# A two-layer mixer network on one core: zeroed weights on another engine, row factors one iteration later, two stores on another queue, and output tokens in chunks of 512, 384 and 256

## The chip, the core and the metric

The kernel runs on one core of a Trainium2 chip. The time is that of the whole program on the device, in microseconds (us). A core has TensorE (PE, matrix multiplications, with its weight loads shown apart as PEld), VectorE (DVE), ScalarE (ACT), GpSimd (POOL) and SyncE (SP), which here issues the transfers. Each of them works through its own list of instructions in order; they wait for one another by semaphores. TensorE's clock has two levels, 1.2 and 2.4 GHz; the profile gives the granted clock of a stretch as a share of the upper one (0.50 is the lower level).

## The reference

Two layers work on 128 context tokens and 1024 latent tokens of width 1024; inside a layer the width is 2048 for `u` and 2048 for `z`. Layer 0 mixes tokens by a Fourier transform, layer 1 by a gated linear recurrence in both directions:

```python
def _layer(x, cond, p, kind, h0):
    shift, scale, gate = _ada(cond, w_ada, b_ada)
    h = _rmsnorm(x, norm_g) * (1.0 + scale) + shift
    u, z = jnp.split(h @ w_in, 2, axis=-1)
    if kind == 0:
        y = _fourier_mix(u, p["w_fmix"], p["b_fmix"])   # real part of an FFT over tokens and 256 channels, then 8 blocks of 256x256
    else:
        ...                                             # convolution, gates, scans in both directions
    out = (y * jax.nn.silu(z)) @ w_out
    return x + gate * out, state
```

After the second layer comes a last RMS norm with the gain `final_g`, which scales each token by one factor.

## The kernel before

Activations lie channel by token: 128 channels on the partitions, 1152 tokens (128 + 1024) along the row. A matrix multiplication in fp32 is three with fp32r operands: `split` makes of a tile a high part (an ACT copy, L227) and a low part (a DVE subtraction, L230), and `mm3` (L240 to L242) multiplies high by high, high by low and low by high.

The program runs through these stages: 0 to 95 us the tables of the Fourier transform; 95 to about 250 us the loop over g (8 groups of 256 channels); then `z` of layer 0 for 16 row blocks and its output stage; then layer 1; from about 1275 us its output stage, which ends the program.

**The loop over g.** `uweights(g + 1)` loads two halves uL and uR of 512 KB (L833, L835), makes their sum `e` and difference (written over uL) on DVE (L838, L839) and splits both into e.h, e.l, o.h, o.l. `umat(g)` multiplies these with the transformed tokens Q into `pu` and copies `pu` out as `uh` (ACT, L870) and `ul` (DVE, L871). `ymat(g - 1)` multiplies the result of the iteration before with two 256x256 blocks (`pa`, which ACT copies to `p`; `qb`), and 16 DVE operations make `y` of `p` and `qb` (L901 to L908), stored as yD (L909). Beside it, at g = 0:

- `prologue()` makes the weights `w8`, which are zero but for some columns, and multiplies them with Q into `nyq` (L797), which goes to `Ucat` (L800) and from there into `pa`.
- `rows()` spreads the tokens' norm factors over the partitions: 9 diagonal tiles `dg` on DVE (L808), three multiplications `rb` (L810), and copies on ACT into the row tile of the same name.
- `norm_stream(c, k)`, 24 times, 4 for each g from 0 to 5: SP loads a tile `nt` of x (L823), POOL scales it with `rb`, shift and scale, and SP stores it to hD (L829). There are 3 buffers for `nt`. The `z` stage loads hD again as `hr`.
- At g = 2, SP stores the vector silT to silD (L928), from where a later load broadcasts it.

An engine's order is the order in which the code calls it, but the tile scheduler reorders what isn't pinned by `keep_in_program_order`. SP is one list: a load behind a store that must wait for POOL waits with it.

**The output stage** (`out_stage`). The tokens are cut into three chunks OC of 384. For each chunk all 16 `g` tiles of 128 channels are loaded as `gr` and split into `gh` and `gl`, and for each of 8 row blocks m the 16 are multiplied with w_out's block in two halves of 8 (tiles `wo`, 512 KB each, split on loading), into one `o` in PSUM. The result times `gate` plus `xr`, the layer's input, is `x` (L1092). Squares are summed over the 8 blocks, three column sums `r` (L1039) are turned into factors (`rsqrt_cols`), three diagonal tiles `dg` (L1045) are spread by one multiplication `b` (L1053), and `to_out` scales and stores the 8 tiles (L1444, L1445). For layer 1 the first 8 steps go through the first half of blocks 0 to 3 and then their second half, so that PE can start before all `g` tiles are there. The split tiles lie in pools of 10 and 26 slots, used in turn.

Of the kernel before, what the change touches and what calls it, by code (L numbers as in the profile page):

```python
# [7 lines left out]
F32 = mybir.dt.float32  # L8
F32R = mybir.dt.float32r
# [10 lines left out]
KD = 8  # L20
DI = 2048
MT = 16
# [3 lines left out]
UC = ((0, 256), (256, 578))  # L26
ENG = {mybir.EngineType.PE, mybir.EngineType.DVE, mybir.EngineType.Activation}
OC = ((0, 384), (384, 768), (768, 1152))
GAP = 3
LB = 30.0  # L30
BO = 60.0
# [156 lines left out]
def body(tc, nc, a):  # L188
# [50 lines left out]
    def mm3(out, wh, wl, xh, xl, first, last):  # L239
        PE.matmul(out, wh, xh, start=first, stop=False)  # L240
        PE.matmul(out, wh, xl, start=False, stop=False)  # L241
        PE.matmul(out, wl, xh, start=False, stop=last)  # L242
# [531 lines left out]
    with pool("us", "right") as up:  # L774
# [6 lines left out]
        def prologue():  # L781

            w8r = up.tile([128, KD, G], F32, name="w8r")
            SY.dma_start(w8r, a["w128"])
            w8f = hl_tiles("w8")[0]
            w8 = w8f.rearrange("p (k n) -> p k n", k=KD)
            zt = up.tile([128, 1024], F32, tag="e", name="zt")
            tc.keep_in_program_order(V.memset(zt, 0.0))
            V.tensor_copy(w8f, zt)
            for o in (0, 32, 64):  # L790
                V.tensor_copy(w8[:, :, o:o + 8], w8r)
                V.tensor_tensor(w8[:, :, o + 8:o + 16], w8r, w8[:, :, 0:8].bitcast(F32), op=ALU.subtract)
            pu = ps2("nyq")
            for i, (lo, hi) in enumerate(UC):
                for k in range(KD):
                    for j in range(2):
                        PE.matmul(pu[i][:, 0:hi - lo], w8[:, k, :], Qc[i][k][j][:, 0, :],  # L797
                                  start=k == 0 and j == 0, stop=k == KD - 1 and j == 1)
                A.copy(Ucat[:, lo:hi], pu[i][:, 0:hi - lo])
                V.tensor_tensor(Ucat[32:64, lo:hi], pu[i][32:64, 0:hi - lo], Ucat[32:64, lo:hi].bitcast(F32), op=ALU.subtract)  # L800
# [113 lines left out]
        for g in range(G):  # L914
            nxt = uweights(g + 1) if g + 1 < G else None
            uv = umat(g, uw)
            if g == 0:
                prologue()
            if prev is not None:
                ymat(g - 1, prev)  # L920
            if g == 0:
                rows()
            for c, k in ns[4 * g:4 * g + 4]:
                norm_stream(c, k)
            prev, uw = uv, nxt
            if g == 2:
                for q in range(2):
                    tc.keep_in_program_order(SY.dma_start(silD[0, q].rearrange("(k p) -> p k", p=128), silT[:, :, q]))  # L928
        zw = {m: wload(a["w_z0"][m], f"wz{m}") for m in range(2)}
        hqb_cm.__exit__(None, None, None)  # L930
        hqa_cm.__exit__(None, None, None)
# [21 lines left out]

    def g_load(layer, c, k, src=None, eng=None):

        lo, hi = OC[c]
        n = c * MT + k
        total = sum(p[1] for p in gpools)
        n %= total
        for p, bufs, rbufs in gpools:  # L960
            if n < bufs:
                break
            n -= bufs
        r = src
        if r is None:
            r = p.tile([128, 384], F32, tag="gr", name=f"gr{layer}{c}{k}", bufs=rbufs)
            SY.dma_start(r, gD[layer][k][:, lo:hi])
        h = p.tile([128, 384], F32R, tag="gh", name=f"gh{layer}{c}{k}", bufs=bufs)
        lw = p.tile([128, 384], F32R, tag="gl", name=f"gl{layer}{c}{k}", bufs=bufs)
        split(r, h, lw, eng)  # L970
        return h, lw

# [54 lines left out]
    def out_stage(layer, op, ow, on_chunk):  # L1027
        order = [(c, m) for c in range(3) for m in range(KD)]
        gt = {}
        pending = []  # L1030
        for k in range(MT):
            gt[0, k] = gt0.get(k) if layer == 0 else g_load(layer, 0, k)

        def norm_steps(c, ssum, xt, last=()):
            def sums():
                pr = ps(f"r{layer}{c}")
                todo = [(t, i) for t in (ssum, *last) for i in range(3)]
                for n, (t, i) in enumerate(todo):
                    PE.matmul(pr[:, 2 * i:2 * i + 2], t[:, i * 128:i * 128 + 128], ones[:, 0:2],  # L1039
                              start=n == 0, stop=n == len(todo) - 1)  # L1040
                r3 = op.tile([128, 3], F32, tag="r3", name=f"r3{layer}{c}", bufs=2)
                rsqrt_cols(r3, pr[:, 0:6:2], op, f"rr{layer}{c}", 3)
                dg = op.tile([128, 384], F32, tag="sq", name=f"dg{layer}{c}", bufs=2)
                for i in range(3):
                    V.tensor_scalar(dg[:, i * 128:i * 128 + 128], ident, r3[:, i:i + 1], None, op0=ALU.mult)  # L1045
                if layer == 1 and c == 2:
                    spread(dg)
                else:
                    pending.append(lambda: spread(dg))

            def spread(dg):
                pb = ps(f"b{layer}{c}")
                PE.matmul(pb[:, 0:384], ones128, dg, start=True, stop=True)  # L1053
                on_chunk(c, xt, pb)
            return sums

        steps = [(c, m, hf) for c, m in order for hf in range(2)]
        if layer == 1:

            steps[0:8] = [(0, m, hf) for hf in range(2) for m in range(4)]  # L1060
        pts = {}
        for n, (c, m, hf) in enumerate(steps):
            lo, hi = OC[c]
            for c2, m2, hf2 in steps[n + 2 if n == 0 else n + 3:n + 4]:
                ow[c2, m2, hf2] = wload(a[f"w_out_{layer}"][m2][:, hf2], f"wo{layer}{c2}{m2}{hf2}")
            if hf == 0:
                pts[m] = ps(f"o{layer}{c}{m}")
            wh, wl = ow.pop((c, m, hf))
            for k8 in range(8):
                k = hf * 8 + k8  # L1070
                ks = slice(k8 * 128, k8 * 128 + 128)
                mm3(pts[m][:, 0:384], wh[:, ks], wl[:, ks], *gt[c, k], k == 0, k == MT - 1)
            if hf == 0:
                continue
            pt = pts.pop(m)
            if m == 0:
                ssum = op.tile([128, 384], F32, tag="ssum", name=f"ssum{layer}{c}", bufs=2)
                xt = []
            xr = op.tile([128, 384], F32, tag="xr", name=f"xr{layer}{c}{m}", bufs=3)
            if layer == 0:  # L1080
                SY.dma_start(xr, a["xT"][m][:, lo:hi])
                add_pos(xr, m, lo, hi)
            else:
                SY.dma_start(xr, x1D[c][m])
            if pending:
                pending.pop(0)()
            if m == KD - 1 and c < 2:
                for k in range(MT):
                    gt[c + 1, k] = g_load(layer, c + 1, k)
            x = op.tile([128, 384], F32, tag="x", name=f"x{layer}{c}{m}", bufs=10)  # L1090
            for s, e, q in segments(lo, hi):
                V.scalar_tensor_tensor(x[:, s - lo:e - lo], pt[:, s - lo:e - lo], gate(layer, m, q), xr[:, s - lo:e - lo],  # L1092
                                       op0=ALU.mult, op1=ALU.add)
            if m == 0:
                A.activation(ssum, x, AF.Square)
            else:
                sq = op.tile([128, 384], F32, tag="sq", name=f"sq{layer}{c}{m}", bufs=2)
                A.activation(sq, x, AF.Square)
                if (layer, c, m) == (1, 2, KD - 1):
                    tail = (sq,)  # L1100
                else:
                    tail = ()
                    V.tensor_tensor(ssum, ssum, sq, op=ALU.add)
            xt.append(x)
            if layer == 0:
                SY.dma_start(x1D[c][m], x)
            if m == KD - 1:
                pending.append(norm_steps(c, ssum, xt, tail))
        return pending
# [327 lines left out]


    with pool("gpa", "right") as ga_, pool("gpb") as gb_, pool("os1") as op:
        gpools[:] = [(ga_, 10, 3), (gb_, 26, 4)]  # L1440
        def to_out(c, xt, pb):
            lo, hi = OC[c]
            for m in range(KD):
                V.scalar_tensor_tensor(xt[m], xt[m], fing[:, m:m + 1], pb[:, 0:384], op0=ALU.mult, op1=ALU.mult)  # L1444
                SY.dma_start(a["yT"][m][:, lo:hi], xt[m])  # L1445

        for step in out_stage(1, op, ow1, to_out):
            step()
# [114 lines left out]
```

## Time and profile before

| | |
|---|---|
| time, median of 3 runs | 1502.44 us (1501.05, 1502.5, 1502.44) |
| profiled execution | 1502.73 us, of which the span of its instructions is 1500.9 |
| PE busy | 1438.3 us, 96% of the span |
| DVE, ACT, POOL busy | 72%, 49%, 9% |
| granted clock of PE, mean | 0.989 |
| moved by DMA | 214.14 MB, 143 GB/s on average |

An engine that is busy all the time sets the time; where PE is this, a change of other engines' work counts only where PE waits for it, or where its clock is low.

### The profile page before, as it was taken

How to read it: one execution, taken by the hardware profiler on the slowest of the kernel's cores; microseconds unless marked ns; L12 is line 12 of the kernel's file. 1: busy time of each engine (PE TensorE's matmuls, PEld its weight loads, DVE VectorE, ACT ScalarE, POOL GpSimd, SP SyncE). 2: the span in 40 equal slices, each digit the busy share in tenths (PEclk: the TensorE clock that was granted, in tenths of full speed). 3: DMA queues.
4: the chain of work that ended last, by engine and by line, in shares of the span. 5: the costliest groups of instructions: out<-in, count | busy, mean ns of one | idle time of the engine just before them, and what ended most of it. 6: DMA issues, size and time to landing. Idle time of an engine off the chain costs nothing. (4 is left out here: it accounts for less than half of the span.)

```text
span 1500.9 us, 21433 instructions
## 1 busy us (share of the span) xinstructions
PE 1438.3 (96%) x8364; PEld 1411.9 (94%) x8364; DVE 1077.3 (72%) x1592; ACT 739.8 (49%) x1109; POOL 128.6 (9%) x148
## 2 busy tenths in 40 slices
PE   3989989999999999999999999999999999999997
PEld 2689889999999999999999999999999999899996
DVE  7886455789864475747888787878787888676453
ACT  6553214322222354426866666666665758354231
POOL 2107570000001001100000000000000000000000
PEclk9999989999999999999999999999999999999998
DMA  7645765877755667631111111111111112786461
GB/s 257 215 152 178 150 216 192 295 249 249 235 196 162 184 186 243 189 127 43 59 59 59 58 59 58 59 59 58 59 59 59 59 59 64 229 278 213 148 189 48
DMA packets 84694, 214.14 MB, mean 143 GB/s; under 512 B 11504, under 2 KB 42736, under 8 KB 84464
## 3 DMA queue, kind: packets, MB, share of 16 engines
q1 hardware_dynamic: 84592, 212.77, 44.1%
q8 instruction: 65, 1.06, 0.3%
q14 instruction: 37, 0.30, 0.1%
HBM read 173.38 MB, written 39.35 MB: 142 GB/s over the span
## 5 line engine op out<-in xcount | busy, mean ns | idle before, releaser
L272 DVE SCALAR_TENSOR_TENSOR sil1j<-wada,sil 128x1024 bf16<-128x1024 f32 x64 | 78.1, 1221 | 9.9 <-DMA wada<-w_ada 9.8
L1278 DVE SCALAR_TENSOR_TENSOR uc<-u,tab,uc 128x1156 f32<-128x1156 f32 (+2 forms) x54 | 69.3, 1288 | 15.7 <-ACT u L1261 14.4
L1337 DVE SCALAR_TENSOR_TENSOR nu<-ga,nu 128x1156 f32<-128x1156 f32 x32 | 43.4, 1358 | 47.1 <-ACT tr L1332 47.1
L1092 DVE SCALAR_TENSOR_TENSOR x<-o,ada,xr 128x128 f32<-128x128 f32 (+1 forms) x64 | 31.6, 513 | 60.1 <-PE o L242 59.6
L1315 ACT ACTIVATE tr<-g,gb 128x386 f32<-128x386 f32 (+1 forms) x96 | 54.7, 584 | 22.0 <-PE g L242 21.0
L227 ACT CAST gh<-gr 128x384 fp32r<-128x384 f32 x80 | 39.7, 511 | 52.4 <-DMA gr<-gD 51.0
L1264 ACT ACTIVATE uc<-u,tab 128x386 f32<-128x386 f32 (+1 forms) x48 | 32.3, 673 | 61.7 <-PE u L242 61.7
L870 ACT CAST uh<-pu 128x256 fp32r<-128x256 f32 (+1 forms) x32 | 12.6, 397 | 100.0 <-PE pu L242 99.7
L230 DVE TENSOR_TENSOR gl<-gr,gh 128x384 fp32r<-128x384 f32 x80 | 42.2, 555 | 26.2 <-ACT gh L227 25.8
L1390 ACT ACTIVATE szz<-zz 128x386 f32<-128x386 f32 (+1 forms) x48 | 23.6, 495 | 72.1 <-PE zz L242 72.1
L771 POOL TENSOR_TENSOR xr<-xr,tab 128x384 f32<-128x384 f32 (+1 forms) x24 | 23.7, 989 | 400.2 <-DMA xr<-xT 353.3
L1315 ACT ACTIVATE ti<-g,gb 128x386 f32<-128x386 f32 (+1 forms) x96 | 51.5, 579 | 5.8 <-PE g L242 5.7
L1360 POOL COPY st<-nu 128x1 f32<-128x1 f32 x16 | 6.8, 426 | 495.5 <-DVE nu L1359 495.4
L1347 DVE SCALAR_TENSOR_TENSOR ti<-ti,uc 128x1156 f32<-128x1156 f32 x32 | 43.4, 1357 | 7.6 <-ACT ti L1315 7.3
L991 ACT ACTIVATE sz<-z 128x384 f32<-128x384 f32 x48 | 23.4, 489 | 49.8 <-PE z L242 34.6
L871 DVE TENSOR_TENSOR ul<-pu,uh 128x256 fp32r<-128x256 f32 (+1 forms) x32 | 14.4, 454 | 41.7 <-ACT uh L870 41.7
L1321 ACT ACTIVATE nu<-tr,sp2p 128x1156 f32<-128x1156 f32 x32 | 43.4, 1357 | 1.2
L1343 DVE SCALAR_TENSOR_TENSOR tr<-ga,tr 128x1156 f32<-128x1156 f32 x32 | 43.5, 1360 | 0.7
L1351 DVE TENSOR_TENSOR ti<-ti,tr 128x1156 f32<-128x1156 f32 x32 | 43.4, 1357 | 0.4
L1325 ACT ACTIVATE ga<-tr,sm 128x1156 f32<-128x1156 f32 x32 | 43.2, 1349 | 0.1
L1362 DVE TENSOR_TENSOR_SCAN nu<-ga,tab,ti 128x1155 f32<-128x1155 f32 x16 | 41.9, 2618 | 0.1
L1359 DVE TENSOR_TENSOR_SCAN nu<-ga,ti 128x1156 f32<-128x1156 f32 x16 | 40.9, 2558 | 0.3
(1812 smaller groups left out, 5550.8 us busy)
## 6 DMA issues: line engine op xcount, KB each, us to landing
wo<-w_out SPq DMA_DIRECT2D x96, 512.0 KB, 4.4
wz<-w_z SPq DMA_DIRECT2D x32, 512.0 KB, 3.6
wada<-w_ada SPq DMA_DIRECT2D x32, 512.0 KB, 4.3
gr<-gD SPq DMA_DIRECT2D x80, 192.0 KB, 4.0
yD<-y SPq DMA_DIRECT2D x16, 576.0 KB, 3.7
zy<-yD SPq DMA_DIRECT2D x16, 576.0 KB, 6.9
wada<-w_adaN SPq DMA_DIRECT2D x16, 512.0 KB, 4.5
wu<-w_u SPq DMA_DIRECT2D x16, 512.0 KB, 3.6
```

The source lines that it names most:

```text
L230: (eng or V).tensor_tensor(lo, src, hi.bitcast(F32), op=ALU.subtract)
L272: V.scalar_tensor_tensor(junk, w, 0.5, sil[:, q, :], op0=ALU.mult, op1=ALU.mult, accum_out=ada[:, layer, mt, q:q + 1])
L1278: V.scalar_tensor_tensor(T["uc", m][:, lo:hi], T[ut][:, lo + t:hi + t], convw[:, m, t:t + 1], T["uc", m][:, lo:hi], op0=ALU.mult, op1=ALU.add)
L1315: A.activation(T[tg, n][:, lo:hi], T["ps", p][:, 0:hi - lo], AF.Tanh, scale=0.5, bias=gb2[:, 2 * d + mat, m:m + 1])
L1321: A.activation(T["nu", n], T["tr", n], AF.Tanh, scale=sp2[:, d, m:m + 1], bias=sp2[:, d, m:m + 1])
L1325: A.activation(T["ga", n], T["tr", n], AF.Exp, scale=sm4[:, d, m:m + 1], bias=sm4[:, d, m:m + 1])
L1337: V.scalar_tensor_tensor(T["nu", n], T["ga", n], 1.0, T["nu", n], op0=ALU.add, op1=ALU.mult)
L1343: V.scalar_tensor_tensor(T["tr", n], T["ga", n], 1.0, T["tr", n], op0=ALU.add, op1=ALU.mult)
L1347: V.scalar_tensor_tensor(T["ti", n], T["ti", n], 1.0, T["uc", m], op0=ALU.add, op1=ALU.mult)
L1351: V.tensor_tensor(ti, ti, T["tr", n], op=ALU.mult)
L1359: V.tensor_tensor_scan(nu, ga, ti, 0.0, ALU.mult, ALU.add)
L1362: V.tensor_tensor_scan(nu[:, 0:L][:, ::-1], ga[:, 0:L][:, ::-1], ti[:, 0:L][:, ::-1], h0[:, 1, m:m + 1], ALU.mult, ALU.add)
```

## The change

It does six things. The zeroing of `w8` and the copies into it move from DVE to ACT, and the tile zt is gone. `rows()` is called at g = 1 and each four `norm_stream` one iteration later. The two silD stores are issued by ACT. In layer 0's output stage the look-ahead of the weights is written another way. In layer 1's output stage the chunks hold 512, 384 and 256 tokens, with tiles 512 wide of which each chunk uses its part; `xr` is loaded in two pieces where a chunk overlaps two of the 384 in which x1D is stored. The pools of split `g` tiles there hold 7 and 20.

```diff
+OUTC = (OC, ((0, 512), (512, 896), (896, 1152)))
...
-            zt = up.tile([128, 1024], F32, tag="e", name="zt")
-            tc.keep_in_program_order(V.memset(zt, 0.0))
-            V.tensor_copy(w8f, zt)
+            A.activation(w8, ident.rearrange("p (o n) -> p o n", o=1).broadcast_to([128, KD, 128]), AF.Copy, scale=0.0)
             for o in (0, 32, 64):
-                V.tensor_copy(w8[:, :, o:o + 8], w8r)
+                A.copy(w8[:, :, o:o + 8], w8r)
...
-            if g == 0:
+            if g == 1:
                 rows()
-            for c, k in ns[4 * g:4 * g + 4]:
+            for c, k in ns[4 * (g - 1):4 * g] if g else ():
                 norm_stream(c, k)
...
-                    tc.keep_in_program_order(SY.dma_start(silD[0, q].rearrange("(k p) -> p k", p=128), silT[:, :, q]))
+                    tc.keep_in_program_order(A.dma_start(silD[0, q].rearrange("(k p) -> p k", p=128), silT[:, :, q]))
...
-        lo, hi = OC[c]
+        lo, hi = OUTC[layer][c]
+        wid, w = 512 if layer else 384, hi - lo
...
-        h = p.tile([128, 384], F32R, tag="gh", name=f"gh{layer}{c}{k}", bufs=bufs)
-        lw = p.tile([128, 384], F32R, tag="gl", name=f"gl{layer}{c}{k}", bufs=bufs)
+        h = p.tile([128, wid], F32R, tag="gh", name=f"gh{layer}{c}{k}", bufs=bufs)[:, 0:w]
+        lw = p.tile([128, wid], F32R, tag="gl", name=f"gl{layer}{c}{k}", bufs=bufs)[:, 0:w]
...
-            for c2, m2, hf2 in steps[n + 2 if n == 0 else n + 3:n + 4]:
+            for c2, m2, hf2 in steps[n + 2 if n == 0 or layer == 0 else n + 3:n + 3 + layer]:
...
-                mm3(pts[m][:, 0:384], wh[:, ks], wl[:, ks], *gt[c, k], k == 0, k == MT - 1)
+                mm3(pts[m][:, 0:hi - lo], wh[:, ks], wl[:, ks], *gt[c, k], k == 0, k == MT - 1)
...
-                SY.dma_start(xr, x1D[c][m])
+                for i, (l, h) in enumerate(OC):
+                    l, h = max(l, lo), min(h, hi)
+                    if l < h:
+                        SY.dma_start(xr[:, l - lo:h - lo], x1D[i][m][:, l - 384 * i:h - 384 * i])
...
-        gpools[:] = [(ga_, 10, 3), (gb_, 26, 4)]
+        gpools[:] = [(ga_, 7, 3), (gb_, 20, 4)]
```

The scheduler settles what this does to the order on each engine; a row gives line, operation, tiles and shape. First DVE in the loop over g, from the low part of e of g = 1 on, before the change:

```order
L230 TENSOR_TENSOR o1l<-uL_1036,o1h 128x1024
L871 TENSOR_TENSOR ul_1_1108<-pu_1_1_1052,uh_1_1107 128x322
L788 MEMSET zt 128x1024
L789 CAST w8h<-zt 128x1024
L791 CAST w8h<-w8r 128x8x8 x3
L838 TENSOR_TENSOR e_1226<-uL_1222,uR_1224 128x1024
L792 TENSOR_TENSOR w8h<-w8r,w8h 128x8x8 x3
L871 TENSOR_TENSOR ul_0_1102<-pu_0_1_1051,uh_0_1101 128x322
L839 TENSOR_TENSOR uL_1222<-uL_1222,uR_1224 128x1024
```

And the same place after it:

```order
L232 TENSOR_TENSOR o1l<-uL_1036,o1h 128x1024
L838 TENSOR_TENSOR e_1166<-uL_1162,uR_1164 128x1024
L871 TENSOR_TENSOR ul_1_1108<-pu_1_1_1052,uh_1_1107 128x322
L792 TENSOR_TENSOR w8h<-w8r,w8h 128x8x8 x3
L839 TENSOR_TENSOR uL_1162<-uL_1162,uR_1164 128x1024
L232 TENSOR_TENSOR e2l<-e_1166,e2h 128x1024
L871 TENSOR_TENSOR ul_0_1102<-pu_0_1_1051,uh_0_1101 128x322
```

The sum `e` of g = 2 now stands directly behind `o1l`, and the subtractions that finish `w8` stand behind it and one `ul`.

PE at the place of `rb`, before the change, between the last `nyq` and the first `pu` of g = 1:

```order
L797 MATMUL nyq_1127<-Qrl,w8h 128x322
L810 MATMUL rb_0_1164<-dg_1166,ones 128x384
L810 MATMUL rb_0_1174<-dg_1176,ones 128x384
L810 MATMUL rb_0_1184<-dg_1186,ones 128x384
L240 MATMUL pu_0_0_1237<-Qoh_170,e1h 128x256
```

And after it, behind the last `qb` of ymat(0):

```order
L242 MATMUL qb_1_1334<-uh_1_1107,Bh 128x322
L243 MATMUL qb_1_1334<-ul_1_1108,Bh 128x322
L244 MATMUL qb_1_1334<-uh_1_1107,Bl 128x322
L810 MATMUL rb_0_1351<-dg_1353,ones 128x384
L810 MATMUL rb_0_1361<-dg_1363,ones 128x384
L810 MATMUL rb_0_1371<-dg_1373,ones 128x384
L242 MATMUL pu_0_0_1424<-Qoh_170,e2h 128x256
```

The three `rb` stand one `umat` and one `ymat` later; on DVE their `dg` stand behind the 16 operations that make `y` of ymat(0).

SP around the loads of g = 7 (uL7, uR7), with the full names of the tiles (hD1_2 belongs to chunk 1 and the channel block 2 of the norm stream), before the change:

```order
L928 DMA silD_117<-silT_196 128x8x1 x2
L829 DMA hD1_2_79<-nt1_4_1843 128x384
L823 DMA nt1_6_1855<-xT 128x384
L829 DMA hD1_2_79<-nt1_5_1849 128x384
L833 DMA uL7_2293<-w_u0 128x1024
L823 DMA nt1_7_1861<-xT 128x384
L823 DMA nt2_0_2056<-xT 128x384
L835 DMA uR7_2295<-w_u0 128x1024
```

And after it:

```order
L829 DMA hD0_3_76<-nt0_7_1619 128x384
L823 DMA nt1_2_1829<-xT 128x384
L829 DMA hD1_0_77<-nt1_0_1817 128x384
L823 DMA nt1_3_1835<-xT 128x384
L833 DMA uL7_2267<-w_u0 128x1024
L829 DMA hD1_0_77<-nt1_1_1823 128x384
L835 DMA uR7_2269<-w_u0 128x1024
L829 DMA hD1_1_78<-nt1_2_1829 128x384
```

silD is gone from SP; on ACT it stands behind the four `p` of ymat(1). uL7 and uR7 stand behind the 9th and 10th hD instead of the 15th.

## Rows read from the trace of the kernel before

**Rows 1.** The page: its head, and PE's busy time.

```profile
span 1500.9 us, 21433 instructions
...
PE 1438.3 (96%) x8364; PEld 1411.9 (94%) x8364; DVE 1077.3 (72%) x1592; ACT 739.8 (49%) x1109; POOL 128.6 (9%) x148
```

**Rows 2.** PE's waits: for whom; us in total, times, longest.

```profile
PE qb L240 <- DVE ul L871: 10.9, 1, 10.9
...
PE nyq L797 <- DVE w8h L792: 2.4, 1, 2.4
...
PE o L241 <- DVE gl L230: 1.5, 1, 1.5
```

**Rows 3.** DVE's timeline, prologue: start us, us, line, operation.

```profile
104.73 0.91 DVE L788 MEMSET zt<- 128x1024 f32 x1 [0.16 <-DVE ul L871]
...
106.82 1.22 DVE L838 TENSOR_TENSOR e<-uL,uR 128x1024 f32<-128x1024 f32 x1
```

**Rows 4.** PE by windows: us, PE busy (matmuls), granted clock, DMA share, GB/s.

```profile
108.58:114.40 5.82, 5.82 (x32) 0.75 0.31 93
114.00:118.00 4.00, 1.74 (x7) 1.00 0.00 0
```

**Rows 5.** Timeline of PE and DVE, `rb` and the end of ymat(0).

```profile
115.85 1.85 DVE L808 TENSOR_SCALAR dg<-tab,rs 128x128 f32<-128x128 f32 x9
...
116.67 2.17 PE L810 MATMUL rb<-dg,ones 128*128 128x384 f32 x6 [2.26 <-DVE dg L808]
...
135.21 0.28 PE L240 MATMUL pu<-Qoh,e2h 128*128 128x256 f32 x1
...
137.79 0.20 DVE L908 TENSOR_TENSOR y<-p,qb 128x63 f32<-128x63 f32 x1
```

**Rows 6.** SP's timeline around silD: start us, us to issue.

```profile
171.62 1.18 SPq L928 DMA_DIRECT2D silD<-silT  x2
...
175.52 0.38 SPq L829 DMA_DIRECT2D hD<-nt  x1
...
185.74 0.38 SPq L835 DMA_DIRECT2D uR<-w_u  x1
```

**Rows 7.** PE by windows, around the long wait.

```profile
176.00:182.00 6.00, 6.00 (x47) 1.00 0.91 23
188.00:200.00 12.00, 5.03 (x22) 0.50 0.61 217
```

**Rows 8.** Tile uL, then line L829: landing, and ns, first and last start.

```profile
DMA to landing us min/median/max: 3.9/4.5/11.2
...
L829 SPq DMA_DIRECT2D hD<-nt x24: 319/326/1022, 124.7 to 221.0; - x24
```

**Rows 9.** Timeline: ACT's `p` of ymat(1), DVE's `e` of g = 6 and 7.

```profile
149.38 1.69 ACT L888 ACTIVATE p<-pa,tab 128x256 f32<-128x256 f32 x4
...
162.49 1.23 DVE L838 TENSOR_TENSOR e<-uL,uR 128x1024 f32<-128x1024 f32 x1 [1.60 <-DMA uR<-w_u]
...
190.70 1.95 DVE L838 TENSOR_TENSOR e<-uL,uR 128x1024 f32<-128x1024 f32 x1 [13.29 <-DMA uR<-w_u]
```

**Rows 10.** PE by windows, start of the last output stage.

```profile
1274.00:1316.00 42.00, 36.73 (x202) 1.00 0.69 222
...
1316.00:1320.00 4.00, 4.00 (x15) 0.57 0.79 230
```

**Rows 11.** PE by windows: matmuls of 512, 256 and 384 columns.

```profile
59.78:62.30 2.52, 2.52 (x12) 1.00 0.95 278
95.04:98.64 3.60, 3.60 (x33) 1.00 0.80 249
...
1340.00:1480.00 140.00, 140.00 (x805) 1.00 0.54 167
```

**Rows 12.** Timeline of the tail: the spread and the final multiplications.

```profile
1491.67 1.65 PE L1053 MATMUL b<-dg,ones 128*128 128x384 f32 x2 [1.94 <-DVE dg L1045]
...
1493.35 4.29 DVE L1444 SCALAR_TENSOR_TENSOR x<-x,tab,b 128x384 f32<-128x384 f32 x8 [1.74 <-PE b L1053]
```

More of the change, by code (lines that the diff above doesn't have):

```diff
@@ L965, in g_load @@
         if r is None:
-            r = p.tile([128, 384], F32, tag="gr", name=f"gr{layer}{c}{k}", bufs=rbufs)
+            r = p.tile([128, wid], F32, tag="gr", name=f"gr{layer}{c}{k}", bufs=rbufs)[:, 0:w]
             SY.dma_start(r, gD[layer][k][:, lo:hi])
-        h = p.tile([128, 384], F32R, tag="gh", name=f"gh{layer}{c}{k}", bufs=bufs)
-        lw = p.tile([128, 384], F32R, tag="gl", name=f"gl{layer}{c}{k}", bufs=bufs)
+        h = p.tile([128, wid], F32R, tag="gh", name=f"gh{layer}{c}{k}", bufs=bufs)[:, 0:w]
+        lw = p.tile([128, wid], F32R, tag="gl", name=f"gl{layer}{c}{k}", bufs=bufs)[:, 0:w]
         split(r, h, lw, eng)
@@ L1029, in out_stage @@
         gt = {}
+        wid = 512 if layer else 384
         pending = []
@@ L1034, in norm_steps @@
         def norm_steps(c, ssum, xt, last=()):
+            nb = xt[0].shape[-1] // 128
             def sums():
                 pr = ps(f"r{layer}{c}")
-                todo = [(t, i) for t in (ssum, *last) for i in range(3)]
+                todo = [(t, i) for t in (ssum, *last) for i in range(nb)]
                 for n, (t, i) in enumerate(todo):
@@ L1040, in sums @@
                               start=n == 0, stop=n == len(todo) - 1)
[L1041 to L1044, printed above, removed]
+                r3 = op.tile([128, nb], F32, tag="r3", name=f"r3{layer}{c}", bufs=2)
+                rsqrt_cols(r3, pr[:, 0:2 * nb:2], op, f"rr{layer}{c}", nb)
+                dg = op.tile([128, wid], F32, tag="sq", name=f"dg{layer}{c}", bufs=2)[:, 0:128 * nb]
+                for i in range(nb):
                     V.tensor_scalar(dg[:, i * 128:i * 128 + 128], ident, r3[:, i:i + 1], None, op0=ALU.mult)
@@ L1052, in spread @@
                 pb = ps(f"b{layer}{c}")
-                PE.matmul(pb[:, 0:384], ones128, dg, start=True, stop=True)
+                PE.matmul(pb[:, 0:128 * nb], ones128, dg, start=True, stop=True)
                 on_chunk(c, xt, pb)
@@ L1062, in out_stage @@
         for n, (c, m, hf) in enumerate(steps):
-            lo, hi = OC[c]
-            for c2, m2, hf2 in steps[n + 2 if n == 0 else n + 3:n + 4]:
+            lo, hi = OUTC[layer][c]
+            for c2, m2, hf2 in steps[n + 2 if n == 0 or layer == 0 else n + 3:n + 3 + layer]:
                 ow[c2, m2, hf2] = wload(a[f"w_out_{layer}"][m2][:, hf2], f"wo{layer}{c2}{m2}{hf2}")
@@ L1076, in out_stage @@
             if m == 0:
-                ssum = op.tile([128, 384], F32, tag="ssum", name=f"ssum{layer}{c}", bufs=2)
+                ssum = op.tile([128, wid], F32, tag="ssum", name=f"ssum{layer}{c}", bufs=2)[:, 0:hi - lo]
                 xt = []
-            xr = op.tile([128, 384], F32, tag="xr", name=f"xr{layer}{c}{m}", bufs=3)
+            xr = op.tile([128, wid], F32, tag="xr", name=f"xr{layer}{c}{m}", bufs=3)[:, 0:hi - lo]
             if layer == 0:
@@ L1089, in out_stage @@
                     gt[c + 1, k] = g_load(layer, c + 1, k)
-            x = op.tile([128, 384], F32, tag="x", name=f"x{layer}{c}{m}", bufs=10)
+            x = op.tile([128, wid], F32, tag="x", name=f"x{layer}{c}{m}", bufs=10)[:, 0:hi - lo]
             for s, e, q in segments(lo, hi):
@@ L1096, in out_stage @@
             else:
-                sq = op.tile([128, 384], F32, tag="sq", name=f"sq{layer}{c}{m}", bufs=2)
+                sq = op.tile([128, wid], F32, tag="sq", name=f"sq{layer}{c}{m}", bufs=2)[:, 0:hi - lo]
                 A.activation(sq, x, AF.Square)
@@ L1439, in body @@
     with pool("gpa", "right") as ga_, pool("gpb") as gb_, pool("os1") as op:
-        gpools[:] = [(ga_, 10, 3), (gb_, 26, 4)]
+        gpools[:] = [(ga_, 7, 3), (gb_, 20, 4)]
         def to_out(c, xt, pb):
-            lo, hi = OC[c]
+            lo, hi = OUTC[1][c]
             for m in range(KD):
-                V.scalar_tensor_tensor(xt[m], xt[m], fing[:, m:m + 1], pb[:, 0:384], op0=ALU.mult, op1=ALU.mult)
+                V.scalar_tensor_tensor(xt[m], xt[m], fing[:, m:m + 1], pb[:, 0:hi - lo], op0=ALU.mult, op1=ALU.mult)
                 SY.dma_start(a["yT"][m][:, lo:hi], xt[m])
```

## The prediction

> **What bounds the kernel now.** I read the page first: TensorE (PE) is busy 96% of the 1500.9 us span [rows 1]. Time can only be won where PE waits, or where its clock has dropped after a wait. So the second view is the list of PE's waits [rows 2]. The longest, before `fold`, is the start of the program, which the change leaves alone. Of the rest, 10.9 us before `qb` and 2.4 before `nyq`, and 2.3 before `rb` [rows 5], lie where the change moves instructions. The third view is the table of windows, for the clock around each wait. I then went through the five parts in the order of the program.
>
> The profiled execution took 1502.73 us, which is 1.83 more than its span and 0.3 above the median of the runs, 1502.44. The sum is made against 1502.73.
>
> **1. The zeroed weights (`w8`) go to ScalarE.** `nyq` waits 2.4 us because on VectorE (DVE) the MEMSET at 104.73 and the casts come first and then `e`, 1.22 us from 106.82 [rows 3], which stands ahead of the subtractions that finish `w8h`. From the start of `e` to that of `nyq` at 108.58 [rows 4] it is 1.76 us. In the changed order `e(2)` stands directly behind `o1l`, and one more `ul` of about 0.45 behind it: 2.2 from `e` to `nyq`. `e` can start where the MEMSET does now, at 104.7, if uR(2) has landed, and did not wait for it at 106.82. So `nyq` starts at 106.9 to 108.6; I take 107.4, since a landing near the middle is as likely as one at either end: −1.2. After the wait the 32 `nyq` matmuls ran at a mean clock of 0.75 for 5.82 us [rows 4], against 0.75 × 5.82 = 4.37 at full clock. The 1.45 lost comes back if the shorter wait leaves the clock at its upper level. The row for that is `rb`: 2.3 us of waiting there, and its window still shows 1.00 [rows 4]. The sum takes 1.2 + 1.4 = **−2.6**; bounds −3 and 0 (uR late, clock down as now). ScalarE's new ACTIVATE and copies cost nothing as long as they lie beside DVE's `e`; without that cover they take the MEMSET's place, 0.9.
>
> **2. `rows()` one iteration later.** This takes the 2.3 us before `rb` away and makes another wait. In the new place the 9 `dg` (1.85 us) stand behind the 16 subtractions and additions of ymat(0). PE is through ymat(0)'s `qb` at 135.21, where the next `pu` starts now, and DVE finishes the last `y` at 137.99 [rows 5]. Three `dg` (0.62) follow, so PE waits some 3.4 us. Against the 2.3 removed that is +1.1. After 2.4 us the clock fell, after 2.3 it did not; 3.4 lies beyond both, so I add one such loss, 1.6. Sum **+2.7**, bounds +1 (clock stays) and +4 (the clock is down for the `pu` behind it too). Queued behind `rb` on PE is `pu` for g = 2.
>
> **3. The silD stores leave SP's queue.** This is the large term. SP issues the two stores at 171.62 in 4-byte pieces. uL(7) leaves right behind the store hD at 175.52, and uR(7) only at 185.74, a stand of 10 us [rows 6]. Between 176 and 182 the DMA engines are 0.91 busy and move 23 GB/s [rows 7]. The slowest uL takes 11.2 us to land, where the median is 4.5 [rows 8]. On DVE `e(7)` waits 13.29 us for uR until 190.70 [rows 9], and behind it and `uL` in order stands the `ul` that PE needs: the 10.9 us before `qb`. From 188 to 200 the clock is 0.50 [rows 7]: PE's 5.03 us of matmuls are worth half of that, 2.5 more. Gross −13.4.
>
> Not all of it comes back. The norm stream begins after `rb`. That started at 116.67 [rows 5]; it will at 135.2 + 3.4 − 7.0 = 131.6, the 7.0 being the 2.6 of part 1 and the 2.26 of wait and 2.17 of work that are gone ahead of it. So the stores hD, of which the first of 24 left at 124.7 [rows 8] and the 15th at 175.52 [rows 6], (175.52 − 124.7)/14 = 3.63 us apart, begin 15 us later, at 139.7. In the changed order uR(7) stands behind hD number 10: 139.7 + 9 × 3.63 = 172.4, in time. uR(6) stands behind number 5, at 154.2, and `e(6)`, which waits for it until 162.49 today with PE right behind, runs as early with the median landing of 4.5. But silD now leaves ACT after the four `p` of ymat(1), which end near 151 [rows 9], just ahead of both. If the packets hold up SP's stream as they do now (the 10 us ahead of uR(7)), uR(6) is issued near 164, `e(6)` starts 6 us late, and the clock falls too (2.5): 8.5. If they only share the engines, nothing. Between 0 and 8.5 I take **+4**, in the middle, for no row shows two queues at work at once. Net **−9.4**, bounds −13.4 and −4.9.
>
> The page "DMA: Bandwidth & Descriptors" of the Trainium skill (section "Issuing engines are not separate DMA queues") speaks against this part: transfers started by different engines run on the same 16 DMA engines and interleave, and another issuing engine only saves the time on the sequencer. The trace agrees so far: what is full from 176 to 182 [rows 7] is the engines, while SP needs 1.18 us to issue the two. By that rule the move alone would be worth those 1.18 us, and the crowding would show wherever the packets now are. That is rival A below.
>
> **4. The start of the last output stage.** From 1274 to 1316 PE works 36.73 of 42.00 us, and from 1316 to 1320 the clock is 0.57 [rows 10]: 5.3 of waiting and 1.7 of clock, 7.0 in all. The first 8 steps run the first four row blocks in both halves, 192 matmuls. At 384 columns one takes 140 us / 803 = 0.174 (of the 805 in the window two reach in from before it), at 512 columns 2.52 / 11 = 0.229 [rows 11]. Needed in that time are 8 weight tiles of 512 KB and 16 `g` tiles of 192 KB, 7.3 MB in 33.4 us = 217 GB/s; after, with 16 of 256 KB, 8.4 MB in 44.0 us = 191 GB/s. The stretch moved 222. So the later waits, where a weight or a `g` tile came late, lose their ground. But the first `gl` now stands behind one more DVE instruction of 1.35 us (L1351), which lengthens today's first wait of 1.5 [rows 2] to about 3. Kept: 3 + 0.5. Sum **−3.5**, bounds −6 and 0.
>
> **5. The stage itself and its tail.** 256 columns take 3.60 / 30 = 0.120 [rows 11], so 0.229 + 0.174 + 0.120 = 0.523 stands against 3 × 0.174 = 0.522: **0**, within 0.8. At the two chunk borders 27 instead of 36 slots hold the split `g` tiles. Tiles 11 to 15 of a new chunk must wait until PE has left tiles 0 to 4 of the old one. PE then has 11 × 3 × 0.229 = 7.6 us of the old chunk and 5.7 of the new one ahead, while five splits take under 3 us. So nothing; without that cover one wait of about 2 with the clock down behind it. In the tail everything that is 384 wide becomes 256: the 8 final multiplications 4.29 → 2.86, the spread `b` 1.65 → 1.10, small ones −0.2 [rows 12]. The stores follow the multiplications. Sum **−2.2**, bounds −1.5 and −2.8. The shifted look-ahead of layer 0 moves one pair of DVE rows and nothing on PE: 0.
>
> **Sum.** −2.6 + 2.7 − 9.4 − 3.5 + 0 − 2.2 = −15.0. 1502.73 − 15.0 = 1487.7, less 0.3 for the median: **1487.5 us**.
>
> **Rivals.**
> A, the crowding moves along: silD holds SP's stream up for the full 10 us at its new place, `e(6)` is 6 us late and the clock falls: 8.5 instead of 4, so 1487.5 + 4.5 = 1492; with the dear bound of part 2 (+1.3) and the output stage's start as slow as now (+3.5), 1497. For it: 0.91 busy at 23 GB/s [rows 7], which no change of the issuing engine removes. Against it: today SP's own stores stand behind silD in one queue, and then they don't. Chance 0.25.
> B, clean: no residual in part 3, and 2.5 more at the start of the output stage: 1487.5 − 6.5 = 1481. For it: uR(6) and uR(7) stand behind hD numbers 5 and 10, due at 154.2 and 172.4, ahead of today's issue. Against it: the time of silD, 151. Chance 0.18.
> C, slower: the small packets on a second queue starve SP's stream instead of sharing with it, and `e(6)` waits for uR(6) longer than `e(7)` does now. Everything but part 3 brings −2.6 + 2.7 − 3.5 − 2.2 = −5.6, so slower by 3 us begins where the residual exceeds 13.4 + 5.6 + 3 = 22 us: `e(6)` at about 182 instead of 162.49, hD number 5 at 175 instead of 154.2, a stand of 21 us against 10 now. For it: SP's stream is already at its latest relative to PE at that place, since it begins 15 us later. Against it: silD's crowding lasted from 171.62 to 182 or so, half of that. Above 1505.5; chance 0.09.
> The forecast's own case, 1484 to 1491, has 0.40. The 0.08 left is a time that can't be told from none: A with waits at the borders of the chunks.
>
> 0.2% (3.0 us) is about what a measurement of this kernel can tell from no change. Faster by more than that 0.83 (the forecast, A and B), within it 0.08, slower 0.09. The range, 1478 to 1500, reaches from B with its bounds to the dear end of A and leaves out C, most of the 0.08 and a tail of B.
>
> **What would show it.** PE's waits after: no 10.9 before `qb`; one before `rb`, of 3 to 4 us, behind `y`; `nyq` under 1.6 us. `e(6)` and `e(7)`: their waits for uR tell A from B. SP's gap after uL(7) gone. Output stage: one wait of 3 us at its start, no clock drop at 1316. The final multiplications 2.9 instead of 4.29 us. The prediction is wrong if the norm stream's delay reaches a later consumer (the `hh` of the z stage), or if the borders of the chunks show waits.

## The result, and the profile after

The changed kernel takes 1492.82 us (median of 6 runs, 1489.78 to 1495.96) against 1501.62 for the kernel before, run beside it: a ratio of 0.9946 with a 95% interval of 0.9932 to 0.9961, about 8 us less. The forecast was 1487.5 with a range of 1478 to 1500. The time lies in the range, but not in the forecast's own case, 1484 to 1491: it is what rival A gave, 1492 to 1497. The profiled execution took 1495.83 us and is one of the longer of the six, so its sum below comes to 6.9 less than that of before.

The head of the page, PE's busy time, and the two queues by which transfers went:

```profile
span 1494.0 us, 21452 instructions
...
PE 1435.5 (96%) x8362; PEld 1393.2 (93%) x8362; DVE 1074.9 (72%) x1587; ACT 740.2 (50%) x1113; POOL 125.2 (8%) x148
...
q1 hardware_dynamic: 84816, 212.76, 44.1%
q10 hardware_dynamic: 2080, 0.01, 0.4%
```

The last line is new: ACT's queue, 2080 packets for 0.01 MB. That is silD. PE's waits, as in [rows 2]:

```profile
PE qb L242 <- DVE ul L871: 10.0, 1, 10.0
...
PE rb L810 <- DVE dg L808: 3.3, 1, 3.3
...
PE o L243 <- DVE gl L232: 2.3, 1, 2.3
...
PE nyq L797 <- DVE w8h L792: 0.7, 1, 0.7
```

The wait before `nyq` has gone from 2.4 to 0.7, the one before `rb` is 3.3, the first `gl` of the last stage costs 2.3 instead of 1.5, all near what was forecast. But a wait of 10.0 us before `qb` is still there. It is not the same one: it now belongs to g = 5, behind `e(6)`. DVE's row for it, beside [rows 9]:

```profile
174.05 1.22 DVE L838 TENSOR_TENSOR e<-uL,uR 128x1024 f32<-128x1024 f32 x1 [13.76 <-DMA uR<-w_u]
```

The timeline of ACT's and SP's queues before it, beside [rows 6]:

```profile
149.75 0.39 ACTq L928 DMA_DIRECT2D silD<-silT  x1
...
150.17 0.59 ACTq L928 DMA_DIRECT2D silD<-silT  x1
...
150.80 0.38 SPq L833 DMA_DIRECT2D uL<-w_u  x1
164.58 0.33 SPq L823 DMA_DIRECT2D nt<-xT  x1
...
167.42 0.38 SPq L835 DMA_DIRECT2D uR<-w_u  x1
```

uL(6) leaves just after silD, as the order said, and then SP stands for 13.8 us. What it waits for is in the list of its own waits from 145 to 170, an `nt` buffer whose store hD doesn't finish:

```profile
SPq L823 <- DMA hD<-nt: 14.9, 2, 13.4
```

uR(6) leaves at 167.42; the estimate was 154.2 undisturbed and 164 held up. The windows, beside [rows 7]:

```profile
152.00:160.00 8.00, 8.00 (x62) 1.00 1.05 11
...
174.00:186.00 12.00, 8.94 (x46) 0.62 0.60 211
```

For 8 us the profile gives the engines a busy share of 1.05 while they move 11 GB/s, and behind the wait PE's clock is again low, 0.62 from 174 to 186. The other places, `rb` and the tail, beside [rows 5] and [rows 12], first the timeline, then the window around `rb`:

```profile
131.00 3.17 PE L810 MATMUL rb<-dg,ones 128*128 128x384 f32 x6 [3.29 <-DVE dg L808]
...
1486.65 0.80 PE L1056 MATMUL b<-dg,ones 128*128 128x256 f32 x2 [1.72 <-DVE dg L1048]
...
1487.49 3.22 DVE L1450 SCALAR_TENSOR_TENSOR x<-x,tab,b 128x256 f32<-128x256 f32 x8 [0.89 <-PE b L1056]
```

```profile
131.00:135.00 4.00, 4.00 (x11) 0.63 0.74 260
```

Behind the wait of 3.3 us before `rb` the clock is down in this execution, as the sum had it.

Where the time came from, by the start of the same instruction in both traces:

| first matmul of | before | after | shift | in this part |
|---|---|---|---|---|
| `pu` of g = 0 | 91.94 | 91.69 | −0.25 | −0.25 |
| `pu` of g = 3 (behind `nyq`, `rb`) | 151.72 | 151.14 | −0.58 | −0.33 |
| `z` (end of the loop over g) | 251.50 | 250.48 | −1.02 | −0.44 |
| `o` of the last stage | 1275.32 | 1273.68 | −1.64 | −0.62 |
| the last matmul of `o` | 1487.24 | 1482.96 | −4.28 | −2.64 |
| end of the span | 1500.9 | 1494.0 | −6.9 | −2.6 |

Most of the gain lies in the last output stage and the tail. The part of the loop from g = 3 on, where −9.4 was forecast for silD alone, gave 0.4.

### The profile page after: what moved, and what is told of

Its sections match the earlier page's. It is cut to its first block, busy times and chain, and to the rows that moved or that the text cites. A ratio compares the mean times of both kernels' runs of the same rounds, so it can differ in the third digit from the quotient of the medians.

```text
span 1494.0 us, 21452 instructions
## 1 busy us (share of the span) xinstructions
PE 1435.5 (96%) x8362; PEld 1393.2 (93%) x8362; DVE 1074.9 (72%) x1587; ACT 740.2 (50%) x1113; POOL 125.2 (8%) x148
## 3 DMA queue, kind: packets, MB, share of 16 engines
q10 hardware_dynamic: 2080, 0.01, 0.4%
## 5 line engine op out<-in xcount | busy, mean ns | idle before, releaser
L1098 DVE SCALAR_TENSOR_TENSOR x<-o,ada,xr 128x128 f32<-128x128 f32 (+2 forms) x64 | 31.6, 513 | 53.5 <-PE o L244 53.0
L229 ACT CAST gh<-gr 128x384 fp32r<-128x384 f32 (+2 forms) x80 | 39.4, 510 | 51.7 <-DMA gr<-gD 50.1
L232 DVE TENSOR_TENSOR gl<-gr,gh 128x384 fp32r<-128x384 f32 (+2 forms) x80 | 42.0, 554 | 28.0 <-ACT gh L229 27.8
L870 ACT CAST uh<-pu 128x256 fp32r<-128x256 f32 (+1 forms) x32 | 12.6, 397 | 95.6 <-PE pu L244 95.5
```

## The experiments

Theory P: silD's 2048 pieces of 4 bytes hold up the other transfers wherever and by whichever queue they are issued. Rival N: the norm stream, which begins later, makes uR(6) late. Rival Q: it matters which queue is used. The first four kernels ran on one chip (the kernel before: 1502.84), the next four on another (1502.49), the last four on a third (1498.71). Most runs of one kernel lie within some 5 us of their median, and the chips differ, so ratios to the kernel before on the same chip are compared.

**1. silD in rows.** silT is turned by one small multiplication and stored as 16 rows of 512 bytes.

```diff
-                for q in range(2):
-                    tc.keep_in_program_order(A.dma_start(silD[0, q].rearrange("(k p) -> p k", p=128), silT[:, :, q]))
+                silQ = up.tile([128, 2, KD], F32, name="silQ")
+                A.copy(silQ, silT.rearrange("p k q -> p q k"))
+                silP = ps("silP")
+                PE.matmul(silP[0:16, 0:128], silQ.rearrange("p q k -> p (q k)"), ident, start=True, stop=True)
+                silW = up.tile([128, 384], F32, tag="nt", name="silW", bufs=3)[0:16, 0:128]
+                A.copy(silW, silP[0:16, 0:128])
+                tc.keep_in_program_order(A.dma_start(silD[0].rearrange("q (k p) -> (q k) p", p=128), silW))
```

> The changed kernel with one edit: silT is copied, turned by one small multiplication with the identity on PE and stored as 16 rows of 512 bytes instead of 2048 pieces of 4 bytes, by ACT at the same place. Theory P (the small packets hold up SP's transfers wherever they are issued): the 10.0 us that PE waits before qb in the changed kernel go, and the low clock behind them (about 2.5), so some 12 us less: about 1481, and no uR takes longer than 7 us to land. Rival N (the later norm stream makes uR(6) late, since it stands behind the fifth hD): the wait stays at 8 us or more and the time within 3 us of the changed kernel, 1490 to 1496.

1480.78 us, ratio 0.9859 (0.9846 to 0.9872): 12 us below the changed kernel, as theory P had it (run 11 below, the same kernel once more, comes out less far down). SP's timeline, then a window of PE, then ACT's copy of the turned rows:

```profile
151.17 0.38 SPq L833 DMA_DIRECT2D uL<-w_u  x1
152.66 0.33 SPq L823 DMA_DIRECT2D nt<-xT  x1
...
153.77 0.42 SPq L835 DMA_DIRECT2D uR<-w_u  x1
```

```profile
152.00:160.00 8.00, 8.00 (x61) 1.00 0.91 299
```

```profile
159.67 0.25 ACT L932 COPY silW<-silP 16x128 f32<-16x128 f32 x1 [8.78 <-DMA hD<-nt]
```

In the order of the changed kernel uR(6) leaves at 153.77, half a us from the 154.2 of the prediction, and in the same 8 us 299 GB/s are moved. No wait before `qb` is left. The norm stream is as late as in the changed kernel, so N falls. One thing differs besides the size of the pieces: the rows leave ACT at 160.0 instead of 150, since silW is one of the three `nt` buffers, and the copy into it waits 8.78 us for a store hD to free one (the turn on PE is done at 152). That the moment alone isn't the cure is for runs 2 and 8 to show, with 4-byte stores at 163.8 and 233.9; none stores them at 160 itself.

**2. silD back on SP's queue.**

```diff
-                    tc.keep_in_program_order(A.dma_start(silD[0, q].rearrange("(k p) -> p k", p=128), silT[:, :, q]))
+                    tc.keep_in_program_order(SY.dma_start(silD[0, q].rearrange("(k p) -> p k", p=128), silT[:, :, q]))
```

> The changed kernel with one edit: the two silD stores back on SP's queue, where they now stand between the eighth hD and uL(7). Theory P: uR(6) comes in time, and uL(7) and uR(7) stand behind the crowd as in the kernel before: a wait of 5 to 11 us before the qb that follows e(7), time within 4 us of the changed kernel, 1489 to 1497. Rival Q (it matters that a second queue is used): without it the wait falls below 3 us, time below 1486, or a second queue was milder and the time rises above 1498.

1495.07 us, ratio 0.9954 (0.9936 to 0.9972), not to be told from the changed kernel's 0.9946. SP's timeline and PE's longest wait behind the start:

```profile
163.79 1.17 SPq L928 DMA_DIRECT2D silD<-silT  x2
...
166.09 0.33 SPq L829 DMA_DIRECT2D hD<-nt  x1
177.50 0.33 SPq L823 DMA_DIRECT2D nt<-xT  x1
177.93 0.99 SPq L833 DMA_DIRECT2D uL<-w_u  x1
...
182.04 0.38 SPq L835 DMA_DIRECT2D uR<-w_u  x1
```

```profile
PE qb L242 <- DVE ul L871: 11.0, 1, 11.0
```

The stand is 11.4 us here, at another place, and the victim is uR(7), as in the kernel before: 11.0 us. Whose queue it is makes no difference that shows in the time, so Q falls too, although the stores also leave 14 us later here. The engines are not full during this stand, as the window shows:

```profile
166.00:177.00 11.00, 11.00 (x84) 1.00 0.47 36
```

A share near 1, as in [rows 7], is thus not needed for SP to stand; the few GB/s are common to both.

**3. `rows()` and the norm stream back in their old iterations,** silD on ACT.

```diff
-            if g == 1:
+            if g == 0:
                 rows()
-            for c, k in ns[4 * (g - 1):4 * g] if g else ():
+            for c, k in ns[4 * g:4 * g + 4]:
```

> The changed kernel with rows() at g = 0 again and the norm stream back in its old iterations; silD stays on ACT. Theory P: the wait of about 10 us stays, since uL(6) and uR(6) are still issued behind silD, and only the dearer wait before rb is won back, 2.7 us: about 1490. Rival N: with the norm stream 13 to 15 us earlier uR(6) and uR(7) come in time, the long wait goes and the time is about 1480.

1493.33 us (12 runs, 1490.61 to 1505.14), ratio 0.9948 (0.9931 to 0.9965). N is out once more: uR(6) still leaves only at 166.54, and from 152 to 160 the engines move 27 GB/s. But the 2.7 didn't come either. PE's waits:

```profile
PE qb L242 <- DVE ul L871: 7.7, 1, 7.7
PE rb L810 <- DVE dg L808: 3.8, 1, 3.8
```

The wait before `qb` is shorter, and the one before `rb` at its old place is 3.8, not 2.26. `nyq` is over sooner here, and PE comes to `rb` sooner.

**4. Three chunks of 384 in the last stage again.**

```diff
-OUTC = (OC, ((0, 512), (512, 896), (896, 1152)))
+OUTC = (OC, OC)
...
-        gpools[:] = [(ga_, 7, 3), (gb_, 20, 4)]
+        gpools[:] = [(ga_, 10, 3), (gb_, 26, 4)]
```

> The changed kernel with the last output stage in three chunks of 384 and pools of 10 and 26 again. Theory: the profiles of before and after put 2.7 us between the start of this stage and its last o and 2.6 in the tail, so 5.3 slower: about 1498. Rival (the stage's gain depends on what comes before it and the tail hides part of it): less than 2.5 us slower, below 1495.5.

1497.8 us, ratio 0.9967 (0.9955 to 0.9978), against 0.9946: about 3 more, between theory and rival, and with these intervals undecided. In its profile the stage and tail take 5.7 us more than in that of the changed kernel (1270.92 to 1496.9, against 1273.68 to 1494.0), hence runs 9 and 10.

**5. silD in rows, in the kernel before** (the edit of run 1, for the stores on SP). It changes queue and moment too: the rows leave ACT at 160.6, where the pieces left SP at 171.62.

> The kernel before with silD turned by PE and stored as 16 rows of 512 bytes on ACT's queue, nothing else. Theory P: the 10.9 us before qb and the low clock behind them go, about 13 us: 1488 to 1491. Rival (the wait before e(7) has its own cause in SP's order of hD, nt and uR(7), and silD only shares it): less than 8 us, above 1494.

1490.27 us, ratio 0.993 (0.991 to 0.9949): the 10.9 us wait and the low clock behind it are worth 10.5 (0.7% of 1502; 8 to 13 by the interval) with the rest of the kernel left as it was. Its profile has no wait before `qb`. By run 2 and the changed kernel, queue and moment alone bring no such gain.

**6. silD in rows, `rows()` and the norm stream back** (the edits of 1 and 3).

> silD in rows as in the first experiment, and rows() with the norm stream back at g = 0. Theory R (the move of rows() is about even, since the earlier nyq only lengthens the wait before rb at its old place): the wait before rb 3.5 to 4 us, time within 2.5 us of the first experiment, 1478.5 to 1483.5. Rival, by the sum as it stood in the prediction (+2.7 for the move): 2.7 faster, about 1478.

1484.62 us, ratio 0.9881 (0.986 to 0.9903). That is above both expectations. Beside run 1 (0.9859) the move of `rows()` would win some 3 us, beside run 11, the same kernel on another chip (0.9891), it would lose 1.5: undecided, and a loss of 2.7 shows in neither. The wait before `rb` is 3.6 in its profile.

**7. `dg` made early:** as run 1, with the nine `dg` at g = 0 and the three `rb` at g = 1.

```diff
+        dgs = {}
+        def row_diags():
+            for c in range(3):
+                dgs[c] = up.tile([128, 384], F32, tag="nt", name=f"dg{c}", bufs=3)
...
         def rows():
...
+                dg = dgs[c]
...
             if g == 0:
                 prologue()
+                row_diags()
```

> silD in rows, rows() at g = 1, but its nine dg made on DVE right behind nyq's Ucat at g = 0, so that they are there when PE comes to rb. Theory: the 3.3 us before rb go, and with them the low clock in rb and the first pu behind it (about 1.7 of PE's time): some 5 us below the first experiment, about 1476. Rival (the nine dg, 1.8 us, now delay uL and o2l or the copies of pu at g = 1, and a wait comes back there): within 2 us of the first experiment.

1480.62 us, ratio 0.9859 (0.9834 to 0.9884), the same ratio as run 1, on another chip: undecided by time. PE's timeline shows that the wait has gone, and the clock has stayed up (2.10 us for the six passes of `rb`, where the changed kernel took 3.17):

```profile
128.74 2.10 PE L816 MATMUL rb<-dg,ones 128*128 128x384 f32 x6
```

**8. The 4-byte stores at g = 7,** on ACT's queue, behind the last weights of the loop.

```diff
-            if g == 2:
+            if g == 7:
                 for q in range(2):
```

> The changed kernel with the 4-byte stores of silD on ACT's queue issued at g = 7 instead of g = 2, when uL(7) and uR(7) have long landed. Theory P: no wait before qb, but the crowd of some 11 us now lies on the loads of the z stage; PE waits 3 to 9 us at its start and the time is 1484 to 1491. Rival (the z stage has enough in hand): no new wait of over 1 us, time 1480 to 1482 as with silD in rows.

1493.5 us, ratio 0.995 (0.9931 to 0.997): nothing won over the changed kernel, and dearer than the 1484 to 1491 expected. PE's waits and two windows:

```profile
PE z L242 <- ACT hh L229: 4.2, 2, 2.7
PE z L243 <- DVE hl L232: 3.7, 1, 3.7
```

```profile
238.00:244.00 6.00, 6.00 (x38) 1.00 0.88 31
244.00:256.00 12.00, 5.66 (x23) 0.74 0.69 221
```

No `qb` waits, but the crowd of 238 to 244 (31 GB/s) delays the loads `hr` of the `z` stage. PE waits there for 2.7 and 3.7 us (the other 1.5 before `hh` comes later and is in most other profiles too), and its clock is 0.74 from 244 to 256. The changed kernel, run 2 and run 8 store the pieces at three places and by two queues and have one price within their intervals: theory P.

**9 to 12, on one chip.** Run 9 is run 1 with the edit of run 4; run 10 is the kernel before with the uneven chunks alone; 11 and 12 are runs 1 and 7 once more.

> silD in rows as in the first experiment, and the last output stage in three chunks of 384 with pools of 10 and 26. Theory: the uneven chunks are worth 5.3 (2.7 at and in the stage, 2.6 in the tail), whatever lies before: 5 us over the first experiment, run beside it here. Rival: they are worth no more than the 3 that the runs of the fourth experiment showed: 2 to 3.5 us over it.

> The kernel before with the uneven chunks of the last output stage and nothing else of the change (w8, rows() and silD as before). Theory: 5.3 less than before, about 1497; with the long wait before qb and the waits before nyq and rb as before. Rival: 2 to 3.5 less, about 1499.5.

> The first experiment once more, beside the others: about 1481.

> The seventh experiment (dg made early) once more, beside the first on the same chip. Theory: the 3.3 us wait and the low clock behind it are gone for good, 2 to 5 us below the first experiment, 1476 to 1479. Rival: what is won there comes back later in the program, within 1.5 us of it.

| run | median us | ratio to the kernel before | interval |
|---|---|---|---|
| 9, silD in rows, chunks of 384 | 1487.99 | 0.9925 | 0.9903 to 0.9947 |
| 10, uneven chunks alone | 1494.53 | 0.9969 | 0.9954 to 0.9983 |
| 11, silD in rows (run 1) | 1482.49 | 0.9891 | 0.9868 to 0.9913 |
| 12, `dg` early (run 7) | 1479.02 | 0.9866 | 0.9843 to 0.9889 |

The uneven chunks are worth 5.5 us by runs 9 and 11, and 4.6 (0.31% of 1498.7) by run 10: theory's 5.3 is the better of the two, though the interval of run 10 takes in the rival's 3.5.

Run 11 is the kernel of run 1, and its ratio is higher by 0.0032. Against the changed kernel's 0.9946, silD in rows is worth 13 us by run 1 and 8 by run 11; the gain stands, its size is known no better than that. In the two profiles, from the first `pu` of g = 0 to the end of the span, it is 12.6 and 13.2.

Run 12 is 3.5 below run 11, inside the expected 2 to 5, but the intervals overlap, and runs 1 and 7 had the same ratio: by time the gain of the early `dg` isn't shown. The profiles speak for it. From the first `pu` of g = 0 to the first `o` of the last stage they take 1168.8 and 1168.3 us in runs 1 and 11, 1164.6 and 1164.7 in runs 7 and 12. Some 0.9 comes back in the last stage, so that over the whole way to the end of the span 2.7 to 3.4 us remain. Run 12 is the shortest of all versions, 1.3% below the kernel before and some 12 us below the changed one, going by ratios.

## Why the prediction came out as it did

**The step that failed is the residual of part 3.** "Between 0 and 8.5 I take +4, in the middle, for no row shows two queues at work at once." By the table of shifts it was 13.0 (−13.4 + 13.0 = −0.4), above the upper bound; counted from the trace, 10.0 of waiting and 8.94 × 0.38 = 3.4 of low clock, 13.4. The gross term was about right: run 5 takes silD's pieces out of the kernel before and gains 10.5, runs 1 and 11 take them out of the changed kernel and gain 13 and 8. The time of the queue was right as well, since without the crowd uR(6) left at 153.77. Wrong was the idea that on a queue of its own silD would hold the loads back less. Three things made the bound itself too low. SP stood 13.8 us, not the 10 taken from [rows 6]. After it came another store hD, which took 2.3 us to issue, so that uR(6) left 13.2 us late. And uR(6) took 6.6 us to land instead of the median 4.5, so that `e(6)` started 11.6 us later than the 162.49 of [rows 9], where 6 was the worst case.

That the time still lies in the range is not owed to part 3. The range reached to the dear end of rival A, and parts 4 and 5 brought most of what was gained, while parts 1 and 2 nearly cancel.

The sentence from the Trainium skill that stood in the prediction (DMA: Bandwidth & Descriptors, "Issuing engines are not separate DMA queues") described the outcome, and its rule was given 0.25. Run 2 agrees with it: ACT's queue or SP's, the time is the same within its interval.

Some sums of the prediction are off without harm. The store at 175.52 is the 14th hD in the trace, not the 15th, so the stores lie 3.91 us apart, and number 5 is due at 155.3. The 7.3 MB in 33.4 us are 220 GB/s, not 217.

**Part 1, −2.6.** Measured −3.0: the start of `nyq` moved by 1.95, of which 0.25 was there before, and its 32 matmuls ran at full clock. This size hangs on one execution. In runs 5 and 10, which have the old `w8`, `nyq` waits 1.7 and 1.6 us instead of 2.4, and its matmuls run at full clock all the same. From the first `pu` to the last `nyq` it is 22.2 us in the trace of before, 20.1 in both of these and 19.1 in the changed kernel: by them the edit is worth 1.

**Part 2, +2.7.** In the two profiles it is +2.7 as well (from −3.27 behind `nyq` to −0.58 at g = 3), with the wait of 3.3 and the low clock as worked out. But the size does not carry beyond these two executions, and the agreement is luck. The 2.26 us without loss of clock, from which the sum started, is the mildest of its kind: the same place shows 3.3, 3.6, 3.6 and 3.8 in the profiles of runs 10, 5, 6 and 3, and `rb` then takes 3.6 to 4.2 us instead of 2.17. Against those the move costs nothing, and runs 3 and 6 show no gain from undoing it. Nor does the length of the wait settle the clock, as the prediction had it (it falls after 2.4 us and more). At the new place the wait is 3.29 us in each profile with late `dg`, and `rb` takes 3.17 to 4.18 us behind it in those of the changed kernel and of runs 1, 4, 8 and 11, but 2.17 in those of runs 2 and 9:

```profile
132.51 2.17 PE L810 MATMUL rb<-dg,ones 128*128 128x384 f32 x6 [3.29 <-DVE dg L808]
```

**Part 4, −3.5, and part 5, 0 and −2.2.** In the profiles −2.6 from the first to the last `o`, and −2.6 for the tail. The later waits of the start have gone, as the bytes needed per us said; the first wait grew to 2.3, not 3. The tail won more than its third: from the last `o` to `b` it is 0.74 less instead of 0.2, and `b` took 0.80 instead of the 1.10 expected, while the multiplications kept 3.22 instead of 2.86. No border of the chunks shows a wait.

**Rival C** needed a stand of 21 us, or 23 with the landing of 4.5 that the prediction uses elsewhere. It was 13.8 in the changed kernel and 16.2 in the profile of run 4, where the stores stand as in the changed kernel.

## What to carry to other kernels

Before a costly transfer is moved to another queue or another time, look at what it is made of. In the traces here SP's queue stood beside 4-byte pieces while 11 to 36 GB/s were moved, with the engines' busy share anywhere from 0.47 to 1.05, and the stall followed the pieces. One matmul that turned 8 KB into rows of 512 bytes was worth 8 to 13 us, while moving the same pieces to three other places gained nothing that shows. A wait that is moved, and the clock behind it, are also to be sized from more than one execution: the wait of 2.26 us in the trace of before was 3.3 to 3.8 in four others, and behind one and the same wait of 3.29 us the clock was down in five profiles and up in two.

## What was not expected of the hardware

Two stores of 4 KB, 2080 packets on their own queue, took 0.4% of the engines' span, which is 6 us of all 16 engines, and yet SP's queue stood 13.8 us beside them and all traffic fell to 11 GB/s for 8 us. The queues in these 8 us (152 to 160) are, in the changed kernel:

```profile
q10 hardware_dynamic: 811, 0.00, 58.7%
q1 hardware_dynamic: 50, 0.08, 46.3%
```

and in run 1, with no silD packet before 160:

```profile
q1 hardware_dynamic: 1034, 2.39, 90.8%
```

The share times 8 us and 16 engines, over the packets, gives an estimate of 0.09 us for a packet of silD and 1.2 us for one of SP's queue, against 0.11 in run 1. So it is not silD's own packets alone that fill the engines: the few packets of SP's queue beside them take some ten times as long. How the engines choose between the two queues, and why SP stood in run 2 with the engines half idle, no run here shows.
